# Splitting the output weights in two steps and re-ordering loads, masked copies, divisions and scans in a hybrid decoder layer on one Trainium2 core

## The chip, the cores and the metric

The kernel runs on one core of a Trainium2 chip. The metric is the device time of one execution in microseconds (us). Before the change it is 283.31 us, the median of 3 runs (282.31 to 283.62).

## What is computed

One layer of a decoder trunk on x of 512 tokens and 1024 channels in float32: an RMS norm, one input projection, three mixers side by side on slices of its columns, SiLU gates, one output projection, a residual and a final RMS norm. The core of the reference:

```python
h = rmsnorm(x, norm_g[l])
p = jnp.einsum('btd,dc->btc', h, w_in[l])
(gq, gk, gv, gz, ggate, dq, dk, dv, dgate, qi, ki, wi, pu, pgate) = split_cols(p)
glog = log_sigmoid(gz @ gla_gate_w2[l] + gla_gate_b[l]) / 16
y_gla = rmsnorm(gla_mixer(gq, gk, gv, glog), gla_norm_g[l]) * silu(ggate)    # chunks of 64, masked
o_dsa = dsa_mixer(dq, dk, dv, qi, ki, wi, rel_bias)                         # top 128 keys per query
y_dsa = o_dsa * silu(dgate)
y_pool = pool_mixer(pu, pool_w[l], pool_scale[l]) * silu(pgate)             # windows 2, 4, 8, 16
x = x + jnp.einsum('btc,cd->btd', concatenate([y_gla, y_dsa, y_pool]), w_out[l])
return rmsnorm(x, final_norm_g)
```

## The kernel before, in words

All large products are made from a high and a low part of each operand (`hi_of` on ScalarE, `lo_of` mostly on VectorE, some on GpSimd), three matmuls for each product: high by high, low by high and high by low. Tokens are in four tiles of 128 (i = 0 to 3). The kernel has three stages.

`open_run` (lines 916 to 1000) makes the norm and the projection of the first 512 columns. Then `project` (line 1006) goes through eleven chunks of the input weights in the order of `CHUNKS`: qd, n1 to n4, dg, pg, c2, c1, pu, c0. A chunk has two or four steps, and after each half step and step `hooks` runs what the table `after` (line 621) lists under that point. So the order of the program is written by hand: each engine works off its own instructions in the order in which the table issues them, and an instruction that waits holds back all that stand behind it on its engine. Last comes `finish` (line 813), written out in the same manner. It ends the attention and makes the output projection.

What hangs in the table and is touched by the change:

- **Scans for the largest indexer scores.** `topk(n, tiles)` (line 451) makes one round for a tile on VectorE: MAX8 into `m8`, then MATCH_REPLACE8 in the scores `scs`. Tiles 1 to 3 have 16 rounds each.
- **Gated linear attention.** `gla_scores(t)` (line 501) makes the chunk scores `pa` on TensorE and moves them into `AT`: two masked copies on VectorE (COPY_PREDICATED) and one plain copy on ScalarE for each of two `pa`. `gla_out(t)` (line 519) multiplies `AT` by the values into `po`.
- **Sparse attention.** For tile i and head pair g: `att_l` (bias on GpSimd), `att_q` (TensorE scores `ps` of queries `QQ` and keys `KK`, `KL`; VectorE adds the bias and finds the extreme, ScalarE makes the exponentials), `att_n` (VectorE reciprocal `ast`, two divisions on GpSimd), `att_t` (TensorE transposes `tpp`, copies `pt`), `att_v` (TensorE `ov`, VectorE `yt`, ScalarE high part `yDh`) and `att_y` (VectorE low part `yDl`). The table names them by letter, tile and pair: "n22" is the division of tile 2, pair 2.
- **Queries and keys.** `take_dqk` (line 359) projects the chunks c2, c1 and c0; `qkr` is the result, `qkh` and `qkl` its high and low part. Transfers from SP's queue (16 in c2, 12 in c1, 8 in c0) put these into `QQ`, `KK` and `KL`.
- **Pooling.** `pool_branch(j)` (line 577) is five instructions on VectorE, two of them running sums (TENSOR_TENSOR_SCAN).
- **Output weights.** Their four chunks wo0 to wo3 are loaded by `load_next` (two transfers of 512 KB each, on SP's queue) and split by `split_out(n, h)` (line 894): for each of two quarters the high part `oh` on ScalarE and at once the low part `ol` on VectorE. In `finish`, `out_part(t, a, e, kinds)` multiplies the three mixers' results (G, P and D) for tile t by columns a to e.

The order of the loads is set in `project` by

```python
            if n < n_in - 1:
                load_next()
```

Of the kernel before, what the change touches and what calls it, by code (L numbers as in the profile page):

```python
# [69 lines left out]
def hybrid_layer(  # L70
# [546 lines left out]
    def phase(n):  # L617
# [495 lines left out]
```

## Time and profile before

| what | before |
|---|---|
| time, median of 3 runs | 283.31 us (282.31 to 283.62) |
| the profiled execution's own time | 285.67 us |
| its span | 283.2 us |
| mean granted TensorE clock over the span | 0.948 |
| busy: TensorE / VectorE / ScalarE / GpSimd | 256.6 / 198.8 / 120.3 / 101.3 us |
| instructions | 4207 |

The span is what the trace covers of the profiled execution; 2.5 us of its own time lie around it. TensorE is busy for most of the span, so what it loses is in two places: stretches in which it has nothing to do, and stretches in which it is busy at the lower of its two clocks (PEclk 0.50 is 1.2 GHz, 1.00 is 2.4 GHz).

### The profile page before, as it was taken

The page shows a single profiled execution, that of the slowest core. Times are in us where ns is not written, and L with a number is a line of the kernel's source. Part 1 is how long each engine was busy: PE and PEld are TensorE (multiplying, and loading weights), DVE is VectorE, ACT ScalarE, POOL GpSimd, SP SyncE. Part 2 cuts the span into 40 slices and gives each one's busy share as a digit, 9 for nine tenths or more (in the row PEclk, how much of TensorE's full clock was granted, in tenths as well). Part 3 has the DMA queues.
Part 4 walks back from the last instruction along what each step waited for, and adds up shares of the span by engine and source line. Part 5 has one row for each costly group of instructions (what it writes and reads, how often), then busy time and mean ns, then how long its engine had stood idle before and what let it go on. Part 6 is the DMA issues. An engine that isn't in the chain of part 4 may idle for free.

```text
span 283.2 us, 4207 instructions
## 1 busy us (share of the span) xinstructions
PE 256.6 (91%) x1498; PEld 212.6 (75%) x1498; DVE 198.8 (70%) x442; ACT 120.3 (42%) x251; POOL 101.3 (36%) x109
## 2 busy tenths in 40 slices
PE   8999999999995999999999299995979876999991
PEld 5778889999995898888888187673755655777890
DVE  3996789999999797698978513977268765454232
ACT  5971486866440832262233422324165661332111
POOL 1752554430570532175330713326235372200010
PEclk9999999999999599999999869998797997999998
DMA  7994212263032302223157970006175000006111
GB/s 259 408 370 141 84 21 75 78 231 105 1 93 78 131 0 76 74 74 83 67 134 168 287 231 0 0 0 167 64 232 206 3 0 0 0 2 222 74 76 74
DMA packets 11780, 31.09 MB, mean 110 GB/s; under 512 B 1600, under 2 KB 1600, under 8 KB 11760
## 3 DMA queue, kind: packets, MB, share of 16 engines
q1 hardware_dynamic: 11328, 30.05, 32.7%
q10 hardware_dynamic: 432, 0.79, 0.7%
q8 instruction: 12, 0.20, 0.3%
q14 instruction: 8, 0.07, 0.1%
HBM read 23.91 MB, written 2.10 MB: 92 GB/s over the span
## 4 chain that ended last, share of the span: by engine, by line
PE 44%; DVE 28%; issue 13%; ACT 5%; DMA 4%; POOL 3%; SPq 0%; POOLq 0%; ACTq 0%; DVEq 0%
PE op L770 10%; DVE scs L459 5%; PE pf L960 4%; DVE m L458 4%; DVE ol L99 3%; PE pn_n L196 3%; DMA QQ<-qkl 3%; ACT L L710 3%; PE pt_c L208 2%; PE pt_c L209 2%; PE pt_c L210 2%; DVE scs L444 2%; DMA wk<-in_w_in 2%; POOL L L719 1%; PE pt_dg L208 1%
## 5 line engine op out<-in xcount | busy, mean ns | idle before, releaser
L719 POOL TENSOR_SCALAR L<-L,ast 128x128 f32<-128x128 f32 (+3 forms) x24 | 14.4, 612 | 53.7 <-DVE ast L717 45.0
L458 DVE MAX8 m<-scs 128x8 f32<-128x256 f32 (+2 forms) x48 | 26.5, 552 | 0.1
L459 DVE MATCH_REPLACE8 scs<-m,scs 128x256 f32<-128x256 f32 (+2 forms) x48 | 26.0, 542 | 0.0
L196 PE MATMUL pn_n<-wh_n,hTh 128*128 128x270 f32 (+1 forms) x128 | 22.6, 301 | 0.0
L196 PE MATMUL pn_n<-wh_n,hTl 128*128 128x270 f32 (+1 forms) x128 | 22.0, 296 | 0.0
L196 PE MATMUL pn_n<-wl_n,hTh 128*128 128x270 f32 (+1 forms) x128 | 21.6, 291 | 0.0
L710 ACT ACTIVATE L<-L,ast 128x128 f32<-128x128 f32 (+3 forms) x24 | 13.3, 556 | 17.3 <-DVE ast L708 16.2
L208 PE MATMUL pt_c<-hTh,wh_c 128*128 128x512 f32 x48 | 20.3, 422 | 0.0
L99 DVE TENSOR_TENSOR ol<-wr_wo,oh 128x512 fp32r<-128x512 f32 x16 | 14.2, 929 | 8.3 <-ACT oh L96 8.3
L210 PE MATMUL pt_c<-hTh,wl_c 128*128 128x512 f32 x48 | 19.8, 413 | 0.0
L209 PE MATMUL pt_c<-hTl,wh_c 128*128 128x512 f32 x48 | 19.8, 413 | 0.0
L196 PEld LDWEIGHTS pn_n<-wh_n,hTh 128*128 128x128 f32 x128 | 19.0, 198 | 0.7 <-issue 0.4
L196 PEld LDWEIGHTS pn_n<-wh_n,hTl 128*128 128x128 f32 x128 | 18.9, 198 | 0.0
L196 PEld LDWEIGHTS pn_n<-wl_n,hTh 128*128 128x128 f32 x128 | 18.6, 195 | 0.0
L99 POOL TENSOR_TENSOR wl_c<-wr_c,wh_c 128x1024 fp32r<-128x1024 f32 x5 | 11.9, 2389 | 14.8 <-PE pt_c L210 10.2
L708 DVE CUSTOM_DVE_ANT_0 L<-ps,L 128x128 f32<-128x128 f32 (+3 forms) x24 | 10.8, 482 | 8.4 <-PE ps L706 7.2
L96 ACT ACTIVATE yDh<-yt 128x128 fp32r<-128x128 f32 x12 | 3.7, 310 | 28.4 <-DVE yt L742 28.4
L706 PE MATMUL ps<-KK,QQ 128*128 128x128 f32 (+3 forms) x24 | 9.2, 392 | 6.8 <-DMA QQ<-qkl 6.8
L954 POOL TENSOR_TENSOR acc<-acc,sqk 128x512 f32<-128x512 f32 x7 | 10.7, 1533 | 10.7 <-ACT sqk L952 10.6
L770 PE MATMUL op<-oh,yDl 128*128 128x512 f32 (+1 forms) x27 | 10.0, 371 | 4.0 <-DVE yDl L99 4.0
L96 ACT ACTIVATE qkh<-qkr 128x512 fp32r<-128x512 f32 x6 | 3.8, 632 | 23.2 <-DVE qkr L369 9.9
L687 POOL TENSOR_TENSOR L<-scs,TB 128x512 f32<-128x512 f32 x9 | 13.0, 1440 | 0.0
(241 smaller groups left out, 711.4 us busy)
## 6 DMA issues: line engine op xcount, KB each, us to landing
wr_wo<-in_w_out SPq DMA_DIRECT2D x8, 512.0 KB, 4.0
wr_c<-in_w_in SPq DMA_DIRECT2D x6, 512.0 KB, 3.4
wr_n<-in_w_in SPq DMA_DIRECT2D x4, 540.0 KB, 7.7
wr_n<-in_w_in SPq DMA_DIRECT2D x4, 536.0 KB, 3.5
xr<-in_x SPq DMA_DIRECT2D x4, 512.0 KB, 6.3
xk<-in_x_t SPq DMA_DIRECT2D x7, 256.0 KB, 5.2
wk<-in_w_in SPq DMA_DIRECT2D x6, 256.0 KB, 5.1
KK<-qkh SPq DMA_DIRECT2D x12, 128.0 KB, 2.5
```

The costliest lines, as they stand in the source:

```text
L99: return (eng or nc.vector).tensor_tensor(dst, src, hi.bitcast(F32), op=ALU.subtract)
L196: mm(ps[:, 0:n], a[:, k, ts_], w[:, k, :], start=(h + part + k == 0), stop=(h == 1 and part == 2 and k == 3))
L208: mm(ps[:, t0:T], c.hi[h][:, k, cs], hTh[h][:, k, t0:T], start=(h + k == 0), stop=False)
L209: mm(ps[:, t0:T], c.hi[h][:, k, cs], hTl[h][:, k, t0:T], start=False, stop=False)
L210: mm(ps[:, t0:T], c.lo[h][:, k, cs], hTh[h][:, k, t0:T], start=False, stop=(h == 1 and k == 3))
L458: nc.vector.max(out=m8, in_=msk[i])
L459: nc.vector.match_replace(out=msk[i], in_to_replace=m8, in_values=msk[i], imm_value=TAKEN)
L687: nc.gpsimd.tensor_tensor(L[:, :, near], msk[i][:, near].unsqueeze(1).to_broadcast([P, 2, 256]), TB[:, 2 * g:2 * g + 2, :], op=ALU.subtract)
L710: nc.scalar.activation(L[:, b, 0:n], L[:, b, 0:n], AF.Exp, bias=st[:, b:b + 1], scale=-1.0, accum_out=st[:, 2 + b:3 + b])
L719: nc.gpsimd.tensor_scalar(L[:, b, 0:n], L[:, b, 0:n], st[:, 4 + b:5 + b], 1.0, op0=ALU.mult, op1=ALU.mult)
L770: mm(outs[t][a][:, 0:e - a], lhs, rhs, start=(first and yi == 0 and rhs is wh and lhs is yh), stop=(last and yi == len(ys) - 1 and lhs is yl))
L960: mm(pns[t], a[:, t * P:(t + 1) * P], w, start=(k + part == 0), stop=(k == KT - 1 and part == 2))
```

## The change

It does these things:

1. `gla_scores`: ScalarE's plain copies are issued ahead of VectorE's masked copies. Tile 0's scores move up by one step, from the end of n3's last step to the end of the step before it; two scan rounds of tile 3 change places around it.
2. In c2 and c1 some rounds of tile 3's scans move to between `qkr` and `qkl`.
3. The load of wo0 moves from the start of c1 to the end of c1's second step, behind the transfers of the queries and keys of that chunk, and stands directly ahead of wo1's.
4. `split_out` becomes `out_high` and `out_low`, and each low part is issued a few steps after its high part.
5. In pu, c0 and `finish` the divisions (n) come ahead of other work, the low parts (y) go to the end of each list, and both calls of `pool_branch` move to the end of their lists.

```diff
         for b, pa in enumerate(pas):
+            nc.scalar.copy(at[0:64, b::2, 64:128], pa[0:64, :, 64:128])
+        for b, pa in enumerate(pas):
             nc.vector.copy_predicated(at[0:64, b::2, 0:64], cm2[0:64], pa[0:64, :, 0:64])
             nc.vector.copy_predicated(at[64:128, b::2, 64:128], cm2[64:128], pa[64:128, :, 64:128])
-            nc.scalar.copy(at[0:64, b::2, 64:128], pa[0:64, :, 64:128])
...
-        ("n3", 1): [partial(topk, 1, 1, 2, 3)],
-        ("n3", 2): [turn_kd, partial(topk, 1, 1, 2)],
+        ("n3", 1): [partial(topk, 1, 1, 2)],
+        ("n3", 2): [turn_kd, partial(gla_scores, 0), partial(topk, 1, 1, 2)],
...
-        ("n3", 3): [partial(gla_scores, 0), *halves("dg1"), silu_gates, partial(topk, 1, 1, 2)],
+        ("n3", 3): [*halves("dg1"), silu_gates, partial(topk, 1, 1, 2, 3)],
...
-        ("c1", 1, "end"): [*halves("c01"), partial(topk, 16, 2, 3), *att("q02")],
+        ("c1", 1, "end"): [lambda: load_next(), *halves("c01"), partial(topk, 16, 2, 3), *att("q02")],
...
-        ("pu", 1, "mid"): [*att("v02", "t12", "q22"), lambda: pool_branch(0)],
-        ("pu", 1): [*att("y02", "n22"), lambda: split_out(0, 0), *att("v12", "l32")],
-        ("c0", 0, "mid"): [*att("y12", "t22", "q32"), lambda: pool_branch(1)],
+        ("pu", 1, "mid"): att("v02", "t12", "l32", "q22"),
+        ("pu", 1): [*att("n22", "y02", "v12"), lambda: out_high(0, 0), lambda: pool_branch(0)],
+        ("c0", 0, "mid"): [lambda: out_low(0, 0), *att("t22", "q32", "y12")],
         ("c0", 0): att("n32", "l01"),
-        ("c0", 0, "end"): [lambda: split_out(1, 0), lambda: load_next(), *att("v22")],
-        ("c0", 1, "mid"): att("y22", "t32", "q01", "l11"),
+        ("c0", 0, "end"): [lambda: out_high(1, 0), lambda: load_next(), *att("v22"), lambda: pool_branch(1)],
+        ("c0", 1, "mid"): [lambda: out_low(1, 0), *att("t32", "q01", "l11", "y22")],
...
+        out_low(0, 1)
+        do("n11", "t01", "q21", "l00", "y32")
+        out_high(1, 1)
         out_part(1, 0, T, "G", first=True)
...
         out_part(1, 0, T, "P")
-        do("y21", "v00", "t31", "n10", "q20", "l30")
-        split_out(3, 1)
+        do("n10", "v00", "t31", "q20", "l30", "y21")
+        out_low(3, 0)
+        out_high(2, 1)
         do("y00")
         out_part(2, 0, T, "P")
         out_part(0, 0, T, "D", last=True)
-        do("v31", "t10", "n20", "q30")
+        do("n20", "v31", "t10", "q30")
+        out_low(2, 1)
+        out_high(3, 1)
         residual(0, 0, T, 0)
+        out_low(3, 1)
         out_part(0, T, D, "GP", first=True)
...
-            if n < n_in - 1:
+            if n not in (n_in - 1, n_in - 3):
                 load_next()
```

Where that puts the instructions, at three places. The rows are in the order of the engine named; square brackets name the semaphores that a row waits for (DMAHW a transfer's, otherwise an engine's).

**VectorE, around tile 0's masked copies.** `m_3` is a scan round's maxima for tile 3, `wl_dg` the low part of a weight chunk. Before:

```order
L458 MAX m_3_3_993<-scs 128x8
L459 MATCH_REPLACE scs<-m_3_3_993,scs 128x512 [waits DVE_49]
L458 MAX m_1_11_1033<-scs 128x8
L459 MATCH_REPLACE scs<-m_1_11_1033,scs 128x256 [waits DVE_49]
L458 MAX m_2_7_1036<-scs 128x8
L459 MATCH_REPLACE scs<-m_2_7_1036,scs 128x384 [waits DVE_49]
L99 TENSOR_TENSOR wl_dg_1053<-wr_dg_739,wh_dg_1052 128x1024 [waits DMAHW6_49,PE_49,Activation_49]
L458 MAX m_1_12_1056<-scs 128x8
L459 MATCH_REPLACE scs<-m_1_12_1056,scs 128x256 [waits DVE_49]
L515 COPY_PREDICATED AT_133<-cm,pa_1073 64x2x64 [waits PE_49]
L516 COPY_PREDICATED AT_133<-cm,pa_1073 64x2x64
```

From the same place in the order, with the change:

```order
L517 COPY_PREDICATED AT_133<-cm,pa_1030 64x2x64 [waits Activation_49]
L518 COPY_PREDICATED AT_133<-cm,pa_1030 64x2x64
L517 COPY_PREDICATED AT_133<-cm,pa_1031 64x2x64 [waits Activation_49]
L518 COPY_PREDICATED AT_133<-cm,pa_1031 64x2x64
L458 MAX m_1_11_1050<-scs 128x8
L459 MATCH_REPLACE scs<-m_1_11_1050,scs 128x256 [waits DVE_49]
L458 MAX m_2_7_1053<-scs 128x8
L459 MATCH_REPLACE scs<-m_2_7_1053,scs 128x384 [waits DVE_49]
L99 TENSOR_TENSOR wl_dg_1070<-wr_dg_739,wh_dg_1069 128x1024 [waits DMAHW6_49,PE_49,Activation_49]
```

Tile 0's masked copies now stand nine rows earlier, and they wait for ScalarE, where ScalarE's copy waited for them.

**SP's queue, the transfers of chunk c1.** Before:

```order
L147 DMA wr_wo00_1686<-in_w_out 128x1024 [waits DMAHW3_49,Pool_49]
L147 DMA wr_wo01_1688<-in_w_out 128x1024 [waits DMAHW4_49,Pool_49]
L376 DMA QQ4_110<-qkh2_1724 64x512 [waits DMAHW5_49,Activation_49]
L376 DMA QQ4_110<-qkl2_1725 64x512 [waits DMAHW6_49,DVE_49]
L376 DMA QQ5_111<-qkh2_1724 64x512 [waits DMAHW7_49]
L376 DMA QQ5_111<-qkl2_1725 64x512 [waits DMAHW0_49]
L382 DMA KK0_112<-qkh3_1763 64x512 [waits DMAHW1_49,Activation_49]
```

With the change (the eight rows of KK0 to KL1 end with these two):

```order
L382 DMA KL1_119<-qkl3_1760 64x512 [waits DMAHW5_49]
L382 DMA KL1_119<-qkl3_1760 64x512 [waits DMAHW6_49]
L147 DMA wr_wo00_1777<-in_w_out 128x1024 [waits DMAHW7_49,Pool_49]
L147 DMA wr_wo01_1779<-in_w_out 128x1024 [waits DMAHW0_49,DVE_49]
L147 DMA wr_wo10_1796<-in_w_out 128x1024 [waits DMAHW1_49]
L147 DMA wr_wo11_1798<-in_w_out 128x1024 [waits DMAHW2_49]
L376 DMA QQ2_108<-qkh1_1987 64x512 [waits DMAHW3_49,PE_49,Activation_49]
```

The two loads of wo0 stood ahead of the four transfers into QQ4 and QQ5; they now stand behind all twelve transfers of c1, with wo1's behind them.

**VectorE, at the end of c0's first step.** `pm` is `pool_branch(1)`, `qkr` the queries of pair 1. Before:

```order
L708 ISA L_1934,ast_1963<-ps_1965,L_1934 128x512 [waits PE_49]
L708 ISA ast_1963 128x1
L582 SCALAR_TENSOR_TENSOR pm<-up 64x512 x2
L585 TENSOR_TENSOR pf_1976<-pm,tab 128x16 [waits DVE_49]
L586 SCALAR_TENSOR_TENSOR pm<-pm,tab,up 128x512 [waits DVE_49]
L588 TENSOR_TENSOR pm<-pf_1976,up 128x16 [waits DVE_49]
L367 SCALAR_TENSOR_TENSOR qkr_1992<-pt_c_1937,rsb 128x512 [waits PE_49]
L717 RECIPROCAL ast_1963<-ast_1963 128x2 [waits Activation_49]
```

With the change:

```order
L710 ISA L_1883,ast_1962<-ps_1964,L_1883 128x512 [waits PE_49]
L710 ISA ast_1962 128x1
L99 TENSOR_TENSOR yDl<-yt_1919,yDh 128x128
L367 SCALAR_TENSOR_TENSOR qkr_1986<-pt_c_1935,rsb 128x512 [waits PE_49]
L719 RECIPROCAL ast_1962<-ast_1962 128x2 [waits Activation_49]
L99 TENSOR_TENSOR qkl_1988<-qkr_1986,qkh_1987 128x512 [waits Activation_49]
L744 TENSOR_TENSOR yt_2014<-ov_2007,dg 128x128 [waits PE_49]
L583 SCALAR_TENSOR_TENSOR pm<-up 64x512 x2
L586 TENSOR_TENSOR pf_2019<-pm,tab 128x16 [waits DVE_49]
L587 SCALAR_TENSOR_TENSOR pm<-pm,tab,up 128x512 [waits DVE_49]
L589 TENSOR_TENSOR pm<-pf_2019,up 128x16 [waits DVE_49]
```

The five instructions of the pooling stood between tile 3's scores and the queries; they now stand behind the queries (`qkr`, `qkl`), the reciprocal of the division and `yt`.

## Rows read from the trace of the kernel before

**Rows 1.** The page's head and its part 1: busy time, share, instructions.

```profile
span 283.2 us, 4207 instructions
PE 256.6 (91%) x1498; PEld 212.6 (75%) x1498; DVE 198.8 (70%) x442; ACT 120.3 (42%) x251; POOL 101.3 (36%) x109
```

**Rows 2.** Waits of TensorE: who waited for whom, total us, times, longest.

```profile
PE ps L706 <- DMA QQ<-qkl: 6.8, 4, 5.1
PE op L770 <- DVE yDl L99: 4.0, 1, 4.0
PE po L530 <- ACT AT L517: 3.2, 2, 3.0
...
PE pp L594 <- DVE yt L742: 1.9, 1, 1.9
```

**Rows 3.** Stretches: length, busy time of each engine, granted clock, DMA share, GB/s.

```profile
88.80:92.00 3.20, 0.23 (x3) 0.19 (x2) 3.11 (x9) 0.26 (x1) 0.00 (x0) 1.00 0.19 38
92.00:100.00 8.00, 7.82 (x61) 7.16 (x61) 6.48 (x18) 6.01 (x12) 4.72 (x5) 0.57 0.33 119
156.00:161.70 5.70, 0.60 (x3) 0.18 (x2) 3.73 (x3) 2.86 (x3) 4.87 (x4) 0.98 1.02 300
161.70:169.00 7.30, 7.01 (x21) 5.70 (x22) 0.92 (x6) 0.99 (x4) 1.22 (x3) 0.55 0.78 216
191.90:197.20 5.30, 2.33 (x13) 1.73 (x13) 4.40 (x8) 2.23 (x6) 4.20 (x4) 0.85 0.62 156
195.00:203.00 8.00, 6.82 (x26) 5.09 (x28) 2.60 (x7) 1.61 (x6) 1.10 (x1) 0.57 0.51 160
...
212.00:217.00 5.00, 4.38 (x8) 2.25 (x9) 3.75 (x10) 2.49 (x8) 3.83 (x4) 0.66 0.78 297
224.00:227.00 3.00, 2.03 (x13) 1.19 (x12) 2.31 (x10) 1.63 (x7) 1.19 (x2) 1.00 0.00 0
...
236.00:240.00 4.00, 4.00 (x24) 3.24 (x25) 0.79 (x3) 0.67 (x2) 0.24 (x1) 0.57 0.00 0
100.00:156.00 56.00, 56.00 (x332) 46.88 (x331) 46.73 (x117) 18.72 (x30) 18.33 (x10) 1.00 0.32 87
...
154.00:236.00 82.00, 66.19 (x320) 48.76 (x318) 50.14 (x120) 33.74 (x86) 34.45 (x40) 0.90 0.35 106
```

**Rows 4.** Timeline around tile 0's masked copies (start, us, instruction, idle before); last, ScalarE's waits.

```profile
82.04 0.34 PE L513 MATMUL pa<-qe,ke 48*64 48x64 f32 x8
85.45 0.68 DVE L458 MAX8 m<-scs 128x8 f32<-128x512 f32 x1
90.81 0.28 DVE L515 COPY_PREDICATED AT<-cm,pa 64x128 f32<-64x128 uint8 x1
91.50 0.26 ACT L517 COPY AT<-pa 64x128 f32<-64x128 f32 x1 [8.71 <-DVE AT L516]
...
ACT AT L517 <- DVE AT L516: 14.0, 7, 8.7
```

**Rows 5.** SP's queue in chunk c1; then transfers by name with their median us to landing.

```profile
154.10 1.03 SPq L147 DMA_DIRECT2D wr_wo<-in_w_out  x2
157.02 1.01 SPq L376 DMA_DIRECT2D QQ<-qkl  x1
...
QQ<-qkl SPq DMA_DIRECT2D x6, 128.0 KB, 2.4
```

**Rows 6.** Timeline of VectorE and GpSimd at the end of c0's first step.

```profile
187.33 2.45 DVE L582 TENSOR_TENSOR_SCAN pm<-up 64x512 f32<-64x512 f32 x2
190.90 0.68 DVE L367 SCALAR_TENSOR_TENSOR qkr<-pt_c,rsb 128x512 f32<-128x512 f32 x1
191.76 0.70 POOL L719 TENSOR_SCALAR L<-L,ast 128x512 f32<-128x512 f32 x1 [5.69 <-DVE ast L717]
```

**Rows 7.** Timeline of VectorE in the last part: pairs of low parts of the output weights.

```profile
206.94 1.29 DVE L99 TENSOR_TENSOR ol<-wr_wo,oh 128x512 fp32r<-128x512 f32 x2 [1.34 <-ACT oh L96]
214.62 2.89 DVE L99 TENSOR_TENSOR ol<-wr_wo,oh 128x512 fp32r<-128x512 f32 x2 [1.25 <-ACT oh L96]
```

More of the change, by code (lines that the diff above doesn't have):

```diff
@@ L656, in hybrid_layer @@
         ("c2", 0, "mid"): [partial(topk, 1, 2, 3)],
-        ("c2", 0): [partial(gla_turn, 3)],
-        ("c2", 0, "end"): [partial(topk, 1, 3)],
+        ("c2", 0): [partial(topk, 1, 3), partial(gla_turn, 3)],
         ("c2", 1, "mid"): [*halves("pu0"), partial(topk, 1, 2, 3)],
-        ("c2", 1, "end"): [late_tiles, partial(topk, 1, 2, 3)],
+        ("c2", 1): [partial(topk, 1, 3)],
+        ("c2", 1, "end"): [late_tiles, partial(topk, 1, 2)],
         ("c1", 0, "mid"): [*halves("pu1"), partial(topk, 1, 2, 3)],
-        ("c1", 0, "end"): [*halves("c00"), partial(topk, 1, 2, 3)],
+        ("c1", 0): [partial(topk, 1, 3)],
+        ("c1", 0, "end"): [*halves("c00"), partial(topk, 1, 2)],
         ("c1", 1, "mid"): [partial(topk, 1, 2, 3)],
-        ("c1", 1): [lambda: nc.gpsimd.memset(up[:, :, 0:16], 0.0), *att("l02", "l12")],
-        ("c1", 1, "end"): [*halves("c01"), partial(topk, 16, 2, 3), *att("q02")],
+        ("c1", 1): [lambda: nc.gpsimd.memset(up[:, :, 0:16], 0.0), *att("l02", "l12"), partial(topk, 1, 3)],
+        ("c1", 1, "end"): [lambda: load_next(), *halves("c01"), partial(topk, 16, 2, 3), *att("q02")],
         ("pu", 0, "mid"): att("n02", "q12"),
         ("pu", 0): att("t02", "n12", "l22"),
-        ("pu", 1, "mid"): [*att("v02", "t12", "q22"), lambda: pool_branch(0)],
-        ("pu", 1): [*att("y02", "n22"), lambda: split_out(0, 0), *att("v12", "l32")],
-        ("c0", 0, "mid"): [*att("y12", "t22", "q32"), lambda: pool_branch(1)],
+        ("pu", 1, "mid"): att("v02", "t12", "l32", "q22"),
+        ("pu", 1): [*att("n22", "y02", "v12"), lambda: out_high(0, 0), lambda: pool_branch(0)],
+        ("c0", 0, "mid"): [lambda: out_low(0, 0), *att("t22", "q32", "y12")],
         ("c0", 0): att("n32", "l01"),
-        ("c0", 0, "end"): [lambda: split_out(1, 0), lambda: load_next(), *att("v22")],
-        ("c0", 1, "mid"): att("y22", "t32", "q01", "l11"),
+        ("c0", 0, "end"): [lambda: out_high(1, 0), lambda: load_next(), *att("v22"), lambda: pool_branch(1)],
+        ("c0", 1, "mid"): [lambda: out_low(1, 0), *att("t32", "q01", "l11", "y22")],
         ("c0", 1): att("n01"),
-        ("c0", 1, "end"): [*att("v32", "q11", "l21"), lambda: split_out(0, 1)],
+        ("c0", 1, "end"): [*att("v32", "q11", "l21"), lambda: out_high(0, 1)],
     }
@@ L819, in finish @@
         out_part(0, 0, T, "G", first=True)
-        do("y32", "t01", "n11", "q21", "l00")
-        split_out(1, 1)
+        out_low(0, 1)
+        do("n11", "t01", "q21", "l00", "y32")
+        out_high(1, 1)
         out_part(1, 0, T, "G", first=True)
-        do("v01", "t11", "n21", "q00", "l31")
-        split_out(2, 0)
+        do("n21", "v01", "t11")
+        out_low(1, 1)
+        do("q00", "l31")
+        out_high(2, 0)
         load_next()
@@ L830, in finish @@
         out_part(2, 0, T, "G", first=True)
-        do("y01")
+        do("n00", "v11", "t21", "y01")
         pool_low()
-        do("v11", "t21", "n00", "q31", "l10")
-        split_out(3, 0)
+        do("q31", "l10")
         out_part(0, 0, T, "P")
-        do("y11", "v21", "t00", "n31", "q10", "l20")
-        split_out(2, 1)
+        out_low(2, 0)
+        do("n31", "v21", "t00", "q10", "l20", "y11")
+        out_high(3, 0)
         out_part(1, 0, T, "P")
-        do("y21", "v00", "t31", "n10", "q20", "l30")
-        split_out(3, 1)
+        do("n10", "v00", "t31", "q20", "l30", "y21")
+        out_low(3, 0)
+        out_high(2, 1)
         do("y00")
@@ L843, in finish @@
         out_part(0, 0, T, "D", last=True)
-        do("v31", "t10", "n20", "q30")
+        do("n20", "v31", "t10", "q30")
+        out_low(2, 1)
+        out_high(3, 1)
         residual(0, 0, T, 0)
+        out_low(3, 1)
         out_part(0, T, D, "GP", first=True)
-        do("y31", "v10", "t20", "n30")
+        do("n30", "v10", "t20", "y31")
         out_part(0, T, D, "D", last=True)
@@ L892, in out_tiles, with out_high @@
         return [S(f"o{hl}{half}{q}", [P, 2, T], F32R) for hl in "hl"]
-    def split_out(n, h):
+    def out_high(n, h):
         part, j = divmod(n, 2)
@@ L899, in split_out, with out_low @@
                 WO[part].append(out_tiles(part, q))
+            hi_of(WO[part][q][0][:, :, cs], chunks[n_in + n].raw[q // 2][:, 2 * (q % 2):2 * (q % 2) + 2, 0:256])
+    def out_low(n, h):
+        part, j = divmod(n, 2)
+        cs = slice(256 * j, 256 * j + 256)
+        for q in (2 * h, 2 * h + 1):
             wh, wl = (w[:, :, cs] for w in WO[part][q])
-            raw = chunks[n_in + n].raw[q // 2][:, 2 * (q % 2):2 * (q % 2) + 2, 0:256]
-            hi_of(wh, raw)
-            lo_of(wl, raw, wh)
+            lo_of(wl, chunks[n_in + n].raw[q // 2][:, 2 * (q % 2):2 * (q % 2) + 2, 0:256], wh)
     def rms_diag():
```

## The prediction

> **What bounds the kernel now.** I read the page's head and part 1 first, then who waited for whom, then the granted clock by stretches, then the timeline where TensorE stops. TensorE is busy 256.6 of 283.2 us [rows 1]; no other engine comes near, so I look for what TensorE loses. The view of its waits names four places worth reading [rows 2]. The stretches show that a stop costs twice: TensorE stands still, and after the longer stops its granted clock is at 1.2 GHz for some microseconds [rows 3]. Lost there is busy time by one less the mean clock. Four losses follow, in order of time.
>
> A: from 88.80 to 92.00 TensorE is busy 0.23 of 3.20 us, so 2.97 are idle; from 92 to 100 it is busy 7.82 at 0.57, which loses 3.4. It waits for `AT`. The scores `pa` were made at 82.04, but VectorE, filled with scans, comes to the masked copies only at 90.81, and ScalarE stands 8.71 us behind these [rows 3, 4].
>
> B: from 156 to 161.7 it is busy 0.60 of 5.70, so 5.1 are idle, waiting for the queries; then 7.01 busy at 0.55 lose 3.2 [rows 2, 3]. Two loads of 512 KB were issued at 154.10, ahead of the queries, whose last transfer was issued at 157.02. TensorE's wait ended only some 5 us after that, where such a transfer lands in 2.4 in the median [rows 5].
>
> D: from 191.9 to 197.2 it is busy 2.33 of 5.30: 2.97 idle. 6.82 busy at 0.57 then lose 2.9 [rows 3]. VectorE was at pooling from 187.33 to 190.90, and both the queries and the reciprocal that the division waits for stand behind it [rows 6].
>
> E: in the last part it waits 4.0 for `yDl` and 1.9 ahead of the pooling's product [rows 2]; the half clock costs 4.00 times 0.43 = 1.7 after the first and 4.38 times 0.34 = 1.5 after the second [rows 3].
>
> **The change part by part.** *Masked copies (A).* They now begin where the row at 85.45 stands, plus four copies of about 0.3: done near 86.7, some 2 us before TensorE asks for them at 88.8 [rows 3, 4]. ScalarE's copy waits only for `pa`, so VectorE should find it done. The two scan instructions that move behind (0.68 each) and the earlier TensorE work lie beside each other: from 100 to 156 TensorE is busy without a gap and VectorE 46.73 of 56, so VectorE has 9.3 us of its own waits to give up before TensorE, 6.4 us earlier, would wait for it [rows 3]. Gain 2.97 + 3.4 = 6.4, less nothing I can name; I take 6.3.
>
> *Loads behind the queries (B).* The last transfer at 157.02 lands by about 159.4 with nothing ahead of it: 2.8 us after TensorE stopped at 156.6. If VectorE gives up more of its waits than TensorE gains by A, and the scans moved between `qkr` and `qkl` fill its wait for ScalarE, nothing is left. Between 0 and 2.8 I take the middle, 1.4. Gain 5.1 - 1.4 + 3.2 = 6.9, with the 0.3 of a second, short wait 7.2. The four loads, 2 MB, now come together; at the 300 GB/s of the stretch in which two of them run [rows 3] they need 7 us, which the whole of chunk pu covers. Without that cover ScalarE would stand at `out_high(0, 0)`.
>
> *Scans later (D).* Queries and reciprocal come up to 190.90 - 187.33 = 3.57 us earlier, more than the wait of 2.97; but `qkr` may then wait for its own product, and the queries still have to be split and moved. Between 0 and half the wait I take 0.8. Gain 2.97 - 0.8 + 2.9 = 5.1. The pooling falls behind `yt` and ahead of tile 3's copy, which TensorE wants only after another half step.
>
> *Two steps for the weights (E).* A low part no longer stands on VectorE directly behind a high part for which it waits 1.25 to 1.34 us [rows 7]. The last such pair stood ahead of tile 0's `yDl`, and its high part behind two exponentials; now an older pair stands there. I take the 4.0 and the 1.7 as gone, and the 1.9 with its 1.5 as staying. New: two pairs of low parts now come after the last scores, needed by the P products of the second half of the columns. Two pairs of 1.29 and the residual (0.68, as the other row of 512 columns in [rows 6]) stand against nine G products, 1.5 us at the 332 in 56.00 of [rows 3]: a wait between 0 and 1.8. I take 1.7, near the upper end, since VectorE has the last scores to do first. Gain 4.0 + 1.7 - 1.7 = 4.0. The earlier divisions count in D; elsewhere I take nothing for them.
>
> *Clock after the new waits.* A wait of 1.9 was followed by half clock, and the 0.97 idle in 224 to 227 was not [rows 2, 3]. The new waits of 1.4 and 1.7 lie between. I let one of the two lose the mean of the five losses above, (3.4 + 3.2 + 2.9 + 1.7 + 1.5) / 5 = 2.5.
>
> *Low parts beside GpSimd.* A pair took 1.29 us at 206.94 and 2.89 at 214.62, in a stretch in which GpSimd is busy 3.83 of 5.00 [rows 3, 7]. All eight pairs at the one are 10.3, at the other 23.1, 12.8 apart. I leave their total as it is, since some pairs move away from GpSimd's biases and some towards them. The Trainium skill, "SBUF — State Buffer", section "SBUF: two separate sides", says that a VectorE instruction with two SBUF inputs and a GpSimd instruction lock each other out of a shared port pair for a whole instruction. By that, low parts set among earlier divisions and biases would be blocked more often, which speaks against this change; by the rule at its fullest the sum would be smaller by some 6 us. The trace agrees that a pair can more than double.
>
> **Sum.** 6.3 + 7.2 + 5.1 + 4.0 - 2.5 = 20.1. The profiled execution took 285.67 us, so it would take 265.6; that execution is 0.8% above the median of the runs shown, so against 283.31 I forecast **263**.
>
> **The rivals.**
>
> *Everything comes.* The new waits cost no clock, and the wait ahead of the pooling's product goes as well: 20.1 + 2.5 + 1.9 + 1.5 = 26.0, so 257. For it: VectorE is busy only 0.79 of the 4.00 us after 236 [rows 3]. Against it: each stop removed leaves VectorE less time. Chance 0.15.
>
> *VectorE becomes the bound in the last third.* It works 50.14 us of the 82 from 154 to 236 [rows 3]; with B, D and E that stretch shrinks to 65.7, and an engine that works in order at three quarters load will often be late. Then D and E bring nothing: 283.3 - 6.3 - 7.2 = 269.8, and with half a clock loss 271. Chance 0.20.
>
> *Low parts beside GpSimd.* All eight pairs run as the one at 214.62; with some of them slow before, I take half of the 12.8 as new: 263 + 6.4 = 269.4; with the clock lost after the longer waits 272. The rule of "SBUF — State Buffer" in the Trainium skill is this case. Chance 0.05.
>
> *The loads were not what held the queries.* VectorE's `qkl` or TensorE's own order would then hold them as before, B brings nothing, and the change does not do what it says there: 263.2 + 7.2 = 270.4. Chance 0.07.
>
> *Slower: VectorE takes over ScalarE's wait.* ScalarE waited 14.0 us in seven pieces for the masked copies [rows 4]. Now the masked copies wait for ScalarE, and behind them on VectorE stand the scans and weight splits that TensorE needs. If those 14.0 us came over whole, A would bring nothing: 263.2 + 6.3 + 14.0 = 283.5, with one more clock loss of 2.5 after a stop 286. It decides from 15.2 us of such waits, nearly 4 for each of four tiles. Against it: `pa` is made at 82.04 and ScalarE needs 0.26 for a copy [rows 4]. Chance 0.03.
>
> **How the numbers follow.** My case, 259 to 268, has 0.50; with "everything comes" at 0.15, VectorE at 0.20, GpSimd at 0.05, the loads at 0.07 and slower at 0.03 that is 1. The range 256 to 272 takes in the first two whole and most of the next three. About 0.5%, 1.4 us, can be told from no change. All cases but the last are faster by more; I leave 0.02 for gains that cancel: faster 0.95, same 0.02, slower 0.03.
>
> **What would show it.** A: no wait of `po` for `AT`, clock 1.00 from 92 to 100. B: the first `ps` waits under 3 us for the queries, and wo0's loads are issued after the last `KL`. D: `qkr` of pair 1 starts ahead of the scans, TensorE waits under 1.5. E: no long wait of `op` for `yDl`, but one of `op` for `ol` ahead of the second half's P products. I am wrong if TensorE's idle time from 154 on falls by less than 8 us, or if the half clock comes back after waits of 1 to 2 us in several places.

## The result and the profile after

| what | before | after |
|---|---|---|
| median of 4 runs each (lowest to highest) | 282.81 us (282.31 to 283.62) | 262.04 us (261.94 to 262.16) |
| the profiled execution's own time | 285.67 us | 262.02 us |
| its span | 283.2 us | 260.2 us |
| mean granted TensorE clock | 0.948 | 0.994 |

The ratio is 0.9263, with an interval of 0.9236 to 0.9291: faster by 20.8 us in the medians and by 23.0 us between the two profiled spans (that of before was an execution 2.9 us above its median). The median of before is 282.81 here, where the forecast went by 283.31, because a fourth run came in. The forecast was 263, the range 256 to 272. Of the runs further down, one execution of u_masked (303.44 us at a granted clock of 0.755, where its others show 0.98 to 0.99) was slowed as a whole and is left out.

The page's head and its part 1, after, to be read beside [rows 1]:

```profile
span 260.2 us, 4199 instructions
PE 245.0 (94%) x1498; PEld 203.8 (78%) x1498; DVE 197.4 (76%) x442; ACT 119.6 (46%) x251; POOL 103.3 (40%) x109
```

TensorE makes the same 1498 matmuls. Its busy time fell from 256.6 to 245.0, 11.6 us, with no matmul left out: that is the half clock that went. Its idle time fell from 26.6 to 15.2, 11.4 us. So half of the gain is the stops themselves and half the slow clock that came after them.

Waits of TensorE after (who waited for whom, us in total, times, longest), to be read beside [rows 2]:

```profile
PE ps L708 <- DMA QQ<-qkl: 2.1, 3, 0.9
PE op L772 <- DVE yDl L99: 1.5, 1, 1.5
PE tpg L571 <- DVE gg L564: 1.2, 1, 1.2
...
PE pp L595 <- DVE ast L710: 0.9, 1, 0.9
PE op L772 <- DVE ol L99: 0.5, 1, 0.5
PE op L772 <- DVE ast L710: 0.4, 1, 0.4
PE pp L595 <- DVE yt L744: 0.4, 1, 0.4
...
PE op L772 <- ACT oh L96: 0.3, 1, 0.3
```

The waits of 5.1, 4.0, 3.0 and 1.9 are gone; none is longer than 1.5. New are the rows with `gg`, the gated values of linear attention, `ol` and `oh` of the output weights, and `ast` (VectorE's reading of scores, after which their place can be written again). The one for `gg` and those for the queries, one by one (start, us, instruction, idle before it and releaser):

```profile
107.05 0.69 PE L571 MATMUL tpg<-ident,gg 128*128 128x128 f32 x3 [1.20 <-DVE gg L564]
153.20 0.30 PE L708 MATMUL ps<-KK,QQ 128*128 128x128 f32 x1 [0.83 <-DMA QQ<-qkl]
180.10 0.30 PE L708 MATMUL ps<-KK,QQ 128*128 128x128 f32 x1 [0.36 <-DMA QQ<-qkl]
181.42 0.30 PE L708 MATMUL ps<-KK,QQ 128*128 128x128 f32 x1 [0.89 <-DMA QQ<-qkl]
```

Stretches after (length, busy time of TensorE, its weight loads, VectorE, ScalarE and GpSimd, granted clock, DMA share, GB/s), to be read beside [rows 3]:

```profile
88.90:96.90 8.00, 8.00 (x90) 7.72 (x89) 7.83 (x19) 2.40 (x7) 4.56 (x3) 1.00 0.41 134
100.00:108.00 8.00, 6.68 (x61) 5.28 (x60) 7.69 (x25) 1.06 (x4) 3.35 (x2) 1.00 0.00 0
151.00:153.70 2.70, 1.87 (x10) 1.39 (x9) 0.90 (x2) 0.87 (x2) 2.70 (x4) 1.00 0.53 124
178.50:182.00 3.50, 2.25 (x16) 1.79 (x15) 3.42 (x4) 0.59 (x1) 3.24 (x2) 1.00 0.78 190
182.00:190.00 8.00, 8.00 (x51) 6.48 (x50) 6.03 (x19) 3.94 (x13) 3.00 (x4) 1.00 0.50 156
214.00:221.00 7.00, 5.76 (x27) 3.73 (x25) 5.11 (x12) 3.75 (x10) 1.21 (x2) 1.00 0.00 0
151.00:221.00 70.00, 63.83 (x354) 47.69 (x352) 50.67 (x127) 34.32 (x92) 35.89 (x44) 1.00 0.40 118
```

The clock is 1.00, 2.4 GHz, in all of them; the 0.55 to 0.66 behind the stops of before are nowhere left. The last row is the stretch that took 82 us before, with 15.8 idle; now 6.2 of 70 are.

Where along TensorE's work the 23.0 us came from (starts and ends of its matmuls in the two timelines; the last 6.2 us after the last product are the same):

| place | before | after | gained so far | the term |
|---|---|---|---|---|
| start of dg | 103.38 | 96.96 | 6.42 | |
| end of c1 | 156.60 | 152.07 | 4.53 | A 4.5 (forecast 6.3) |
| start of pu | 163.10 | 153.48 | 9.62 | |
| end of c0's first step | 188.12 | 175.09 | 13.03 | B 8.5 (7.2) |
| end of c0 | 202.55 | 184.69 | 17.86 | D 4.8 (5.1) |
| end of the last product | 277.01 | 254.03 | 22.98 | E 5.1 (4.0) |

The clock loss after new waits, forecast at 2.5, did not come.

### The profile page after: what moved, and what is told of

It is laid out like the page before. It is cut to its first block, busy times and chain, and to the rows that moved or that the text cites. A ratio compares the mean times of both kernels' runs of the same rounds, so it can differ in the third digit from the quotient of the medians.

```text
span 260.2 us, 4199 instructions
## 1 busy us (share of the span) xinstructions
PE 245.0 (94%) x1498; PEld 203.8 (78%) x1498; DVE 197.4 (76%) x442; ACT 119.6 (46%) x251; POOL 103.3 (40%) x109
## 4 chain that ended last, share of the span: by engine, by line
PE 47%; DVE 36%; issue 6%; ACT 4%; DMA 3%; POOL 2%; SPq 1%; POOLq 0%; ACTq 0%; DVEq 0%
PE op L772 11%; DVE scs L459 8%; DVE m L458 6%; PE pf L973 5%; DVE ol L99 3%; PE pt_c L210 2%; PE pt_c L208 2%; PE pt_c L209 2%; DVE pm L583 2%; PE ov L741 2%; DMA wk<-in_w_in 2%; PE tpp L730 2%; ACT L L712 2%; DVE wl_n L99 2%; DVE wlk L99 2%
## 5 line engine op out<-in xcount | busy, mean ns | idle before, releaser
L196 PE MATMUL pn_n<-wh_n,hTh 128*128 128x270 f32 (+1 forms) x128 | 21.6, 291 | 0.0
L196 PE MATMUL pn_n<-wh_n,hTl 128*128 128x270 f32 (+1 forms) x128 | 21.0, 286 | 0.0
L208 PE MATMUL pt_c<-hTh,wh_c 128*128 128x512 f32 x48 | 19.3, 402 | 0.0
L209 PE MATMUL pt_c<-hTl,wh_c 128*128 128x512 f32 x48 | 18.9, 394 | 0.0
L196 PEld LDWEIGHTS pn_n<-wh_n,hTl 128*128 128x128 f32 x128 | 18.0, 189 | 0.0
L744 DVE TENSOR_TENSOR yt<-ov,dg 128x128 f32<-128x128 f32 x12 | 3.4, 285 | 13.2 <-PE ov L741 13.2
L99 POOL TENSOR_TENSOR wl_n<-wr_n,wh_n 128x1080 fp32r<-128x1080 f32 (+1 forms) x4 | 10.1, 2536 | 7.1 <-ACT wh_n L96 5.1
L778 ACT ACTIVATE sqo<-xr 128x512 f32<-128x512 f32 (+1 forms) x8 | 4.8, 604 | 16.9 <-DVE xr L777 10.6
L558 POOL TENSOR_TENSOR gss<-gss,hneg 128x4 f32<-128x4 f32 x4 | 4.1, 1014 | 21.4 <-DVE gss L557 21.4
L99 DVE TENSOR_TENSOR ol<-wr_wo,oh 128x512 fp32r<-128x512 f32 x16 | 11.2, 744 | 1.3 <-ACT oh L96 1.3
```

The costliest lines, as they stand in the source:

```text
L99: return (eng or nc.vector).tensor_tensor(dst, src, hi.bitcast(F32), op=ALU.subtract)
L196: mm(ps[:, 0:n], a[:, k, ts_], w[:, k, :], start=(h + part + k == 0), stop=(h == 1 and part == 2 and k == 3))
L208: mm(ps[:, t0:T], c.hi[h][:, k, cs], hTh[h][:, k, t0:T], start=(h + k == 0), stop=False)
L209: mm(ps[:, t0:T], c.hi[h][:, k, cs], hTl[h][:, k, t0:T], start=False, stop=False)
```

## The experiments

**One part alone, and all but one.** Each of the four parts was put alone into the kernel before (s_), and taken alone out of the changed kernel (u_). The edits, shown as the part puts them in; s_masked and u_masked:

```diff
         for b, pa in enumerate(pas):
+            nc.scalar.copy(at[0:64, b::2, 64:128], pa[0:64, :, 64:128])
+        for b, pa in enumerate(pas):
...
-            nc.scalar.copy(at[0:64, b::2, 64:128], pa[0:64, :, 64:128])
...
+        ("n3", 2): [turn_kd, partial(gla_scores, 0), partial(topk, 1, 1, 2)],
```

s_loads and u_loads:

```diff
-            if n < n_in - 1:
+            if n not in (n_in - 1, n_in - 3):
...
+        ("c1", 1, "end"): [lambda: load_next(), *halves("c01"), partial(topk, 16, 2, 3), *att("q02")],
```

s_scans and u_scans (both calls of the pooling to the ends of later lists; shown for the second):

```diff
-        ("c0", 0, "mid"): [*att("y12", "t22", "q32"), lambda: pool_branch(1)],
+        ("c0", 0, "mid"): [*att("y12", "t22", "q32")],
...
-        ("c0", 0, "end"): [lambda: split_out(1, 0), lambda: load_next(), *att("v22")],
+        ("c0", 0, "end"): [lambda: split_out(1, 0), lambda: load_next(), *att("v22"), lambda: pool_branch(1)],
```

s_steps and u_steps (the lists of `finish` with the divisions first, and the low parts a step behind the high ones and at c0's last point; the other lists of pu and c0 stay as they are):

```diff
-        split_out(1, 1)
+        out_low(0, 1)
+        do("n11", "t01", "q21", "l00", "y32")
+        out_high(1, 1)
```

> The kernel before with the masked copies alone changed: ScalarE's plain copies first, tile 0's scores one step earlier, two scan rounds exchanged. Theory 1 (each stop of TensorE has its own cause, so each part brings its share alone): the wait for AT at 89 to 92 and the half clock behind it go, less the new wait of 1.2 us for gg that the changed kernel shows at 107: about 4.5 us off, 278.3. Theory 2 (VectorE is the common bound, and what one stop gives the next takes back): the wait for the queries grows by what was won, 281 to 283.

> The kernel before with the loads of wo0 alone moved behind the transfers of chunk c1. Theory 1: the last query transfer lands near 159.4 in place of 161.7, so TensorE's wait falls from 5.1 to 2.8 us; with half clock behind it as before 2.3 us off (280.5), without it 5.5 (277.3). Theory 2 (the loads were not what held the queries): no change, 282 to 283.

> The kernel before with both calls of the pooling moved to the end of their lists and nothing else. Theory 1: the waits of 3.0 us at 192 to 197 fall under 1 and the half clock behind them goes: 4 to 5 us off, 278 to 279. Theory 2: the wait comes back at tile 3's copy or ahead of the pooling's product: 281 to 283.

> The kernel before with the last part alone changed: high and low parts of the output weights in two steps there, and that part's new order of divisions and low parts. Theory 1: the wait of 4.0 us for yDl and the 1.7 of half clock behind it go, new waits of 1 to 2 come: 4 to 5 us off, 278 to 279. Theory 2: VectorE has no time left there and the wait only changes its name: under 2 us off, 281 or more.

> The changed kernel with the masked copies put back as before (order of the copies, place of tile 0's scores, scan rounds). Theory 1 (own cause): the wait for AT and its half clock return, 4.5 us lost: 266.5. Theory 2 (VectorE the common bound): later stops take up part of it, under 2 us lost: 264 or less.

> The changed kernel with the loads of wo0 back ahead of the query transfers. Theory 1: the wait for the queries goes from 0.8 back to about 5 us and brings the half clock of some 3 us with it: 7 to 8 us lost, 269 to 270. Theory 2 (the scan rounds moved between qkr and qkl did it): under 3 us lost, 265 or less.

> The changed kernel with both calls of the pooling back at their earlier places. Theory 1: 4 to 5 us lost, half of it half clock after the wait for the queries of pair 1: 266 to 267. Theory 2: the earlier divisions and low parts hide most of it, under 2 us lost.

> The changed kernel with the last part in its old order, each low part directly behind its high part again. Theory 1: the wait for yDl of some 4 us and half clock behind it return: 4 to 5 us lost, 266 to 267. Theory 2: with VectorE further ahead there now, the old order costs little: under 2 us lost.

The re-ordered lists of pu and c0 and the scan rounds moved in c2 and c1 are in none of the s_ kernels and in all of the u_ kernels. They were never tried by themselves.

Measured. The kernel before was 283.29 beside the first four and 283.33 beside the others; the gains alone are against the first, the losses against 262.04 (u_masked: three runs):

| part | alone | ratio to before | gain alone | without it | ratio to before | loss without |
|---|---|---|---|---|---|---|
| masked copies | 280.62 | 0.9827 to 0.9961 | 2.7 | 265.0 | 0.9268 to 0.9411 | 3.0 |
| loads | 279.1 | 0.9795 to 0.9905 | 4.2 | 267.43 | 0.9378 to 0.9501 | 5.4 |
| scans of the pooling | 283.18 | 0.9949 to 1.0011 | 0.1 | 268.28 | 0.94 to 0.9513 | 6.2 |
| steps | 276.15 | 0.9696 to 0.9823 | 7.1 | 267.86 | 0.9343 to 0.9495 | 5.8 |
| sum | | | 14.1 | | | 20.4 |

The four parts alone add up to 14.1 of the 20.8 us. The other 6.7 belong to what the parts do together and to the lists that were not tried by themselves; how much to which is not shown. That the losses add up to nearly the whole gain is not a sign that the parts are independent.

Against what was expected: s_scans came out by its theory 2. s_masked lies between its two theories, though the waits for the queries grew only from 5.39 to 5.65 us. s_loads lies inside its theory 1. s_steps gained 7.1 us where 4 to 5 were expected. u_loads lost 5.4 where 7 to 8 were expected, u_masked 3.0 where 4.5 were, u_scans 6.2 and u_steps 5.8 where 4 to 5 were.

What follows, part by part. *Masked copies*: up to the end of c1 they give alone what they give in the whole. With them alone dg starts at 96.86 and c1 ends at 152.00, in the changed kernel at 96.96 and 152.07. So the 1.9 us that are lost again between dg and the end of c1 are lost by this part itself, and not to another one.

*Loads*: alone, the long wait for the queries fell from 5.1 to 1.55, while the short one behind it grew from 0.27 to 0.93; with the old order in the changed kernel the long one was 4.19. In s_loads, then in u_loads:

```profile
157.38 0.30 PE L706 MATMUL ps<-KK,QQ 128*128 128x128 f32 x1 [1.55 <-DMA QQ<-qkl]
158.73 0.30 PE L706 MATMUL ps<-KK,QQ 128*128 128x128 f32 x1 [0.93 <-DMA QQ<-qkl]
...
156.18 0.45 PE L708 MATMUL ps<-KK,QQ 128*128 128x128 f32 x1 [4.19 <-DMA QQ<-qkl]
```

The loads were most of what held the queries, and less in the queue than on the way: s_loads issues the last of these transfers at 156.17, only 0.85 us earlier than before, but TensorE goes on 2.56 us after that issue (158.73), where it was 5.62 before (162.64 after 157.02).

*Steps*: alone, the wait for `yDl` fell from 4.0 to 1.46, and the 1.9 ahead of the pooling's product went, which the expectation had not counted. Taken out, both came back, 3.98 and 1.90, with 1.61 for a copy `pt`.

*Scans*: they are the odd row, nothing alone and the largest loss when undone. TensorE's waits of the two kernels that differ in them show two causes. In s_scans (starts, us, instruction, idle before it and releaser), around the end of c0's first step:

```profile
192.69 0.66 PE L728 MATMUL tpp<-ident,L 128*128 128x128 f32 x4 [0.49 <-POOL L L719]
193.93 0.30 PE L706 MATMUL ps<-KK,QQ 128*128 128x128 f32 x1 [0.59 <-DMA QQ<-qkl]
195.20 0.30 PE L706 MATMUL ps<-KK,QQ 128*128 128x128 f32 x1 [0.86 <-DMA QQ<-qkl]
...
223.41 0.44 PE L739 MATMUL ov<-pt,dv 128*64 128x128 f32 x4 [1.62 <-ACT pt L730]
```

Alone, the pooling's move takes away one of the four waits that made the 2.97 idle us of term D, and three, 1.94 us together, stay. At the last row a wait has grown that was 0.77 before. Four kernels together show why neither half of D does much by itself (waits of TensorE around the end of c0's first step; from that end to the end of c0; granted clock in the worst 4 us behind the waits):

| kernel | pooling | rest of the change | waits, us | to the end of c0, us | clock |
|---|---|---|---|---|---|
| before | early | without | 2.98 | 14.43 | 0.50 |
| s_scans | late | without | 1.94 | 12.41 | 0.63 |
| u_scans | early | with | 2.61 | 12.96 | 0.57 |
| changed | late | with | 1.25 | 9.60 | 1.00 |

Either one alone leaves waits that half clock followed; with both there is none. The trace of s_scans shows 2.0 us gained here, 0.85 of it lost again at the grown wait; why its ten runs show only 0.1 stays open, and the one profiled execution of before was 2.4 us slower than its median of 283.29. In u_scans, in the view of TensorE's starts, and then its stretches there:

```profile
216.61 0.50 PE L772 MATMUL op<-oh,yDl 128*128 128x512 f32 x1 [1.41 <-DVE yDl L99]
...
222.51 0.79 PE L772 MATMUL op<-oh,yGh 128*128 128x512 f32 x1 [2.86 <-DVE xr L777]
```

```profile
218.00:222.00 4.00, 1.65 (x12) 1.06 (x8) 3.38 (x9) 2.50 (x7) 0.00 (x0) 1.00 0.00 0
222.00:226.00 4.00, 3.49 (x9) 2.82 (x10) 1.73 (x4) 1.25 (x4) 1.36 (x2) 0.57 0.00 0
```

The 2.86 us stand 40 us behind the pooling, where the order of no instruction differs. What differs is what the product tile `op` of tile 0's second half has to wait for. In u_scans it is the residual `xr`, which reads the products of the first half; in the changed kernel it is `ast`, the reading of the last scores:

```profile
215.98 0.50 PE L772 MATMUL op<-oh,yGh 128*128 128x512 f32 x1 [0.44 <-DVE ast L710]
```

So the second half was given the first half's place (its bank of PSUM) in u_scans, and that of the scores in the changed kernel. The profile shows the releasers and not the banks. The half clock (0.57) came on top.

**u_scans_bank: the residual earlier in u_scans.**

```diff
         out_part(0, 0, T, "D", last=True)
+        residual(0, 0, T, 0)
         do("n20", "v31", "t10", "q30")
         out_low(2, 1)
         out_high(3, 1)
-        residual(0, 0, T, 0)
```

> The changed kernel with the pooling in its old places, as in u_scans (268.28), and with the residual of tile 0 issued on VectorE directly behind TensorE's D products of the first half, ahead of the last scores and two pairs of low parts. In u_scans the product tile of the second half of tile 0 was given the same PSUM bank as that of the first half, and TensorE waited 2.86 us there for the residual, with the clock at 0.57 in the 4 us behind it. Theory 1, most of what u_scans lost is this wait for a bank and its half clock, not the pooling's time on VectorE: the wait is gone, about 2.86 + 1.5 us less, 263.5 to 265. Theory 2, the pooling's 3.6 us ahead of the queries are the loss, and VectorE is late by as much wherever the residual stands: 267 to 268.5.

Measured: 265.91 us (265.14 to 266.47), ratio 0.9326 to 0.9409. The wait for `xr` is gone from the list of TensorE's waits:

```profile
PE ps L708 <- DMA QQ<-qkl: 2.8, 3, 1.1
PE op L772 <- DVE yDl L99: 1.4, 1, 1.4
PE tpg L571 <- DVE gg L564: 1.2, 1, 1.2
...
PE op L772 <- ACT oh L96: 1.0, 1, 1.0
```

So 2.4 of the 6.2 us were that wait with its half clock, and neither theory holds alone: the other 3.9 are the pooling's place. From the end of c0's first step to the end of c0 TensorE takes 12.85 us here and 9.60 in the changed kernel, which is 3.3 of them.

**Three attempts at a better kernel.** Each is an edit of the changed kernel, and the kernel before was 284.06 beside them. v_last moves one low part ahead of a pair of weights:

```diff
+        do("y00")
         out_low(3, 0)
         out_high(2, 1)
-        do("y00")
```

> The changed kernel with tile 0's low part yDl of the last head pair issued ahead of a pair of low parts of the output weights (2.13 us) instead of behind it. Theory 1, the 1.46 us that TensorE waits there are that pair alone, and VectorE, which then waits 1.55 us for TensorE, has room for the pair: 1.4 us less, 260.6. Theory 2, VectorE is the bound from 208 to 222 us (busy 4.00 of 4.00 in 208 to 212 and 3.62 of 4.00 in 216 to 220), so the waits behind it (0.44, 0.28, 0.52) grow by what is gained: 261.5 to 262.1.

Measured: 260.88 us (260.55 to 261.12), against 262.04 (261.94 to 262.16): 1.2 us less, and as much less than v_queries below, which ran beside it. The wait for `yDl` fell from 1.46 to 0.22, and the waits behind it (0.43, 0.26, 0.52) did not grow. It is the fastest kernel of this study.

v_queries issues both high parts of the queries ahead of both low parts:

```diff
-                for dst, src in ((QQ[2 * g][0:64], ah[0:64]), (QQ[2 * g][64:P], al[0:64]),
-                                 (QQ[2 * g + 1][64:P], ah[64:P]), (QQ[2 * g + 1][0:64], al[64:P])):
+                for dst, src in ((QQ[2 * g][0:64], ah[0:64]), (QQ[2 * g + 1][64:P], ah[64:P]),
+                                 (QQ[2 * g][64:P], al[0:64]), (QQ[2 * g + 1][0:64], al[64:P])):
```

> The changed kernel with the four transfers into QQ in another order: both high parts ahead of both low parts, so that the second high part goes out while VectorE still makes the low part. Theory 1, the queue's time to issue decides, and 0.5 us of it lie idle between the first high and the first low part in c0: TensorE's wait for the last transfer falls from 0.89 to about 0.4 there, 0.1 in c1, and 261.4 comes out. Theory 2, a transfer's own way to memory decides or the first pair of transfers is now late instead: no difference, 261.9 to 262.2.

Measured: 262.13 us (262.07 to 262.18), no gain. The second wait in c0 fell from 0.89 to 0.25, but the first rose from 0.36 to 0.86, and the pooling's product then waited 1.58 where it had waited 0.43 and 0.93.

v_all has both, and moves a scan round of tile 3 from n4 to pg:

```diff
-        ("n4", 2): [partial(gla_norm, 0), partial(topk, 1, 1, 2, 3)],
+        ("n4", 2): [partial(gla_norm, 0), partial(topk, 1, 1, 2)],
...
-        ("pg", 0): [partial(gla_norm, 3), partial(gla_turn, 2), *halves("c10"), partial(topk, 1, 3)],
+        ("pg", 0): [partial(gla_norm, 3), partial(gla_turn, 2), *halves("c10"), partial(topk, 2, 3)],
```

> The changed kernel with both of the above, and with one scan round of tile 3 moved from n4's third step to pg's first, which brings VectorE 1.45 us earlier to the gated values that TensorE waits 1.2 us for at 107 us. Theory 1, each of the three waits is a single late instruction: 0.5 + 1.4 + 1.2 less, about 259. Theory 2, VectorE is full in these stretches and each wait comes back at the next place: 261 or more.

Measured: 261.83 us (260.82 to 263.68), no better than v_last. The wait for `gg` is gone and TensorE ends c1 1.47 us earlier, at 150.60, but then it waits 2.04 for the queries and starts pu at 153.48, to the hundredth where it did:

```profile
152.63 0.30 PE L708 MATMUL ps<-KK,QQ 128*128 128x128 f32 x1 [2.04 <-DMA QQ<-qkl]
```

SP's queue and VectorE show why. In the changed kernel (start, us, transfers):

```profile
138.34 2.44 SPq L382 DMA_DIRECT2D KK<-qkh  x4
...
146.03 2.77 SPq L382 DMA_DIRECT2D KL<-qkl  x4
148.92 0.53 SPq L376 DMA_DIRECT2D QQ<-qkh  x1
...
150.78 0.59 SPq L376 DMA_DIRECT2D QQ<-qkl  x1
```

And in v_all:

```profile
138.34 2.44 SPq L382 DMA_DIRECT2D KK<-qkh  x4
...
148.93 1.17 SPq L376 DMA_DIRECT2D QQ<-qkh  x2
```

From 138.34 on the queue issues twenty transfers, about 0.65 us from one to the next and with no gap over 0.13, and it begins when VectorE has delivered `qkr` (at 136.96 in both kernels). VectorE in turn works without a wait from 131 to 147.9 in both. It comes to the `qkr` of these queries at 147.19 and 147.20, and their low part is ready at 149.3. The queue issues the first low part at 149.55 in the changed kernel and, behind both high parts, at 150.20 in v_all. So VectorE, which did not come earlier by a round moved, and the queue are within 0.3 us of each other in the changed kernel. Which of them would hold the queries without the other was not tried.

## Why the prediction was right, step by step

The time came out within 1 us of the forecast, and the sum within 2.9 of the 23.0 us between the two profiles. What had to show itself did: no wait of `po` for `AT` and clock 1.00 behind it; the first wait for queries under 3 us (0.83), with wo0 issued behind the last `KL`; in c0 waits of 0.36 and 0.89 in place of 3 us; a wait of `op` for `ol` (0.52); idle time from 154 on less by 9.6 us, more than the 8 asked for; no half clock after any of the new waits.

*A was too high by 1.8.* The start was as reckoned: VectorE begins the copies at 85.70 and ends them near 86.95, two us ahead of `po`; dg starts 6.42 us earlier. ScalarE made its copies at 80.02, so VectorE did not take over its 14.0 us of waiting (no wait for `AT` is left in its list) and the slower rival is dead. The step that failed is "VectorE has 9.3 us of its own waits to give". These waits were summed over 56 us, and the work that counts lies in the first 10 of them. In the kernel before VectorE ends `gg` at 107.86, 3.9 us ahead of the `tpg` that needs it (VectorE, then TensorE):

```profile
106.87 0.99 DVE L563 SCALAR_TENSOR_TENSOR gg<-po,gss,gg 128x96 f32<-128x96 f32 x4
111.78 0.49 PE L570 MATMUL tpg<-ident,gg 128*128 128x128 f32 x3
```

So 3.9 was there to give, and not 9.3. In the changed kernel VectorE is busy 7.69 of the 8 us from 100 to 108 and begins `gg` only 0.51 earlier, behind two scan rounds:

```profile
106.36 0.99 DVE L564 SCALAR_TENSOR_TENSOR gg<-po,gss,gg 128x96 f32<-128x96 f32 x4
```

TensorE is 6.09 us ahead of the kernel before just in front of this stop and 4.53 behind it, and stays 4.5 ahead to the end of c1. So 1.6 of the 1.9 us are this stop, and 0.3 were lost just ahead of it, at products of `po` that took 1.35 where they had taken 1.03. v_all then shows that this stop was worth nothing: the queries came when they came.

*B was too low by 1.3.* The residual wait was taken at 1.4 and was 0.83; the stop and the half clock are gone. Another 0.5 is a wait for a division in c0's first step, which the prediction did not count and which went too. Before:

```profile
183.28 1.11 PE L728 MATMUL tpp<-ident,L 128*128 128x128 f32 x6 [0.51 <-POOL L L719]
```

The last transfer was issued at 150.78, 1.3 us before TensorE ended c1, where it was issued 0.4 after that before.

*D was right at 4.8 for 5.1.* The waits that stay are 0.36 and 0.89, where 0.8 was taken. VectorE starts `qkr` at 175.41, ahead of the scans at 177.89:

```profile
175.41 0.69 DVE L367 SCALAR_TENSOR_TENSOR qkr<-pt_c,rsb 128x512 f32<-128x512 f32 x1
176.27 0.17 DVE L719 RECIPROCAL ast<-ast 128x2 f32<-128x2 f32 x1 [0.18 <-ACT L L712]
...
177.89 2.79 DVE L583 TENSOR_TENSOR_SCAN pm<-up 64x512 f32<-64x512 f32 x2
```

But the reason given was too narrow: the pooling's move alone brought about nothing, and the rest of the change without it left 2.61 us of waits there. D is both together. That it is the earlier divisions among the rest is argued from the waits for `L`, which are gone only with both; the divisions were not tried by themselves.

*E was too low by 1.1, for several reasons.* The wait for `yDl` did not vanish but stayed at 1.46, behind one pair of low parts (VectorE, and two biases of GpSimd that ran beside it):

```profile
208.75 1.30 POOL L689 TENSOR_TENSOR L<-scs,TB 128x512 f32<-128x512 f32 x1
208.85 1.34 DVE L99 TENSOR_TENSOR yDl<-yt,yDh 128x128 fp32r<-128x128 f32 x1
210.01 1.09 POOL L693 TENSOR_TENSOR L<-scs,TB 128x512 f32<-128x512 f32 x1
210.11 2.13 DVE L99 TENSOR_TENSOR ol<-wr_wo,oh 128x512 fp32r<-128x512 f32 x2
212.17 0.28 DVE L99 TENSOR_TENSOR yDl<-yt,yDh 128x128 fp32r<-128x128 f32 x1
```

v_last moved that pair and got the 1.2 us. The first `yDl` took 1.34 us beside a bias where the second, with none, took 0.28, and the pair took 2.13 where others took 1.29: 1.9 us, more than the wait. Whether the wait would go with the two biases elsewhere was not tried. In return the wait ahead of the pooling's product, which the sum left standing at 1.9 and its 1.5 of half clock, went to 0.43 and 0.93 at full clock, and the new wait ahead of the second half's P products, taken at 1.7, was 0.28 and 0.52.

*The clock after new waits, -2.5, did not come*: the largest term of the sum that was wrong. Nor did VectorE become the bound of the last third; it has 50.67 us of work in 70.

*Low parts beside GpSimd*, taken at no change, became cheaper. The group on the page, after:

```profile
L99 DVE TENSOR_TENSOR ol<-wr_wo,oh 128x512 fp32r<-128x512 f32 x16 | 11.2, 744 | 1.3 <-ACT oh L96 1.3
```

It was 14.2 us before, 929 ns each, with 8.3 us of waiting for `oh`. What the pairs had beside them explains the difference. Those that ran beside a bias of GpSimd took 2.14 to 2.89 us; there were three before (at 214.62, 227.65 and 233.44) and there is one after, 2.13 at 210.11. Those with nothing beside them took 1.28 or 1.29. Three ran beside divisions: they took 1.27 to 1.69, and the two divisions beside each 2.02 to 2.31, where others of these sizes took 1.15 and 1.37. The Trainium skill's rule of the shared port ("SBUF — State Buffer", "SBUF: two separate sides") is that the two engines lock each other out for a whole instruction. The trace agrees with it at these rows. What the rival had wrong is where the pairs would fall: fewer of them lie beside biases in the new order, not more, and the cost of the one that does is in E.

That the forecast lay so near is partly luck. The sum alone gave 265.6, 3.6 above the profiled execution; it was set against the median of before, 2.4 us below the execution that it came from, and that makes up for most of the 2.5 that did not come. The errors of A against B and E cancel.

## What to carry to other kernels

A stop of the engine that bounds the kernel costs twice where its clock falls after it, so the price of a stop is read from the stretch behind it too. An engine's own waits are slack only at the place where they lie: sum them over the stretch in which the work is needed, not over a stage. And a part tried alone can show nothing where other stops stand right behind it, or change what a product far behind has to wait for; the two-sided trial, alone and all but one, tells.

## What was not expected of the hardware

Waits near 2 us go either way. The 1.9 us ahead of the pooling's product were followed by the 0.66 of [rows 3] in the kernel before, and by 0.61 and 0.71 at their lowest in s_masked (1.82) and s_loads (1.79). s_scans has the same wait of 1.91 and no loss, and u_steps, where it is 1.90 and ends at 195.32, has none either:

```profile
192.00:196.00 4.00, 1.97 (x11) 1.28 (x11) 2.58 (x11) 2.93 (x9) 1.06 (x4) 1.00 0.73 246
196.00:200.00 4.00, 4.00 (x22) 2.49 (x21) 2.75 (x4) 1.82 (x6) 3.68 (x4) 1.00 0.73 298
...
220.00:224.00 4.00, 4.00 (x21) 3.28 (x18) 1.49 (x5) 0.66 (x2) 1.01 (x2) 0.50 0.00 0
```

Its last row stands behind a wait of 3.98. No single wait of 1.46 or less lost the clock in the changed kernel, while in u_scans four short ones in a row between 180 and 185 (0.19, 0.44, 1.07 and 0.91) were followed by 0.76 from 186 to 190.

The price of the same stop differs from execution to execution. s_loads, s_scans, s_steps and the kernel before issue the same work up to dg, with the same wait of 2.97 or 2.98 for `AT`, yet dg starts at 102.61, 103.38, 101.81 and 103.38, with a granted clock of 0.79, 0.51, 0.91 and 0.50 from 96 to 100. The spread is 1.6 us. The Trainium skill, "TensorE: Matmul & The Clock Gate", Part 1, says of a kernel's start that the number of matmuls at the low clock varies between runs of one kernel. The trace agrees, here behind a stop in mid-kernel. So it fits that the changed kernel, without any such stop, lies within 0.22 us in four runs, where the four of before lie within 1.3, and that v_all, with a wait of 2.04, lies within 2.9: its mean clock is 0.997 in the profiled execution of 260.82, without a loss behind that wait, and 0.981 in that of 263.68, of which there is no trace.
